# A transformer layer on one core: branch B's sums as a list of small jobs, its last additions as accumulating transfers, and another order of its products

## The chip, the cores and the metric

The kernel runs on one core of a Trainium2 chip. TensorE (PE) multiplies matrices and transposes, VectorE (DVE) and ScalarE (ACT) work element by element, GpSimd (POOL) here issues transfers, and SyncE (SP) issues most of the loads. The metric is the device time of one execution in microseconds (us).

## The reference

One layer of a streaming encoder: 512 positions, width 2048, float32. Two branches, gated DeltaNet attention (A) and a convolution module (B), are mixed by learned gates; then come an output product and a per-layer embedding. What matters here is the middle:

```python
u = jax.nn.silu(layernorm(u, ln_g[i], ln_b[i])) * jax.nn.silu(z_b)
y_b = u @ w_br_b[i]
...
gate_a, gate_b = jnp.split(jax.nn.sigmoid(gate_logits + b_gate[i]), N_BRANCHES, axis=-1)
mixed = (gate_a * y_a + gate_b * y_b) @ w_out[i]
x = x + rmsnorm(mixed, g_post[i])
```

Here `u` and `y_b` are 512 x 2048, and both weights 2048 x 2048.

## The kernel before

**Numbers.** Every float32 operand of a product is split into a high part (a rounded copy, made by ScalarE: L126 for weights, L1303 for activations, L1553 for the output's weights) and a low part (what is left, a subtraction on VectorE: L127, L1305, L1554). A product is three matmuls: low activations by high weights and high by low, beside high by high (L1415, L1417, L1419 in branch B; L1572 to L1574 in the output stage).

**Seven products for eight.** Branch B, as the gates and the output product, multiplies 2 x 2 blocks with seven products instead of eight (P1, P2, P3, Q4, Q5, P6, P7), by sums of blocks. Sums of weights (`wb_sums`, `wo_sums`) were formed earlier in the run. Sums of activations (S1 to S4, each of four tiles 128x512) are formed by VectorE from the normalised tiles `ur` at the end of `layer_norm` (L1262, into `usf`) and split by L1303 and L1305. A half of the 2048 output columns is a `jp`, 0 or 1, so there are 14 products, each of 48 matmuls of 128x512: eight weight pieces (a high and a low part of 128x512), by two blocks of 128 positions, by three matmuls.

**Order.** `b_job` queues a product, or two that take turns piece by piece. The program before runs P1 of both halves together, then P2 of both, Q4 of both, then for each half Q5, P6, P7, P3. After every matmul of a product `tick()` advances generators that are spawned beside the products: `norm` (the layer norm and the sums, resumed by it every fourth tick, and run to its end by `finish("norm")` ahead of the first Q5) and `mix`. The weights are prepared some pieces ahead. The engines run their own queues in program order.

**Results.** A product's two results lie in PSUM tiles `yp`, all from `yps`, a pool of four banks. When a product ends, its function is called at once and issues all its work in a row: `snap_b` copies a result to SBUF (L1429, ScalarE), `tt_b` adds and subtracts results (L1433, VectorE), and `fin_b` multiplies a finished result by the gate (L1291) and adds it into the mix (L1294). The mix is 16 tiles of 128x512, `gt` in the trace, and already holds branch A's part (L1158, `evac_ya`, which evicts branch A's last results). The `gate_in` function loads the gates (L1287, SP).

**Turning the mix.** `mix` transposes the finished mix for the output product: `turned` (L1318, four transposes of 128x128 on TensorE into `tp`), `combine_low` for the low half of the columns (it forms the operand `ah`, `al` and the sum `sf`, L1333 and L1334) and `combine_high` for the high half (L1303, L1305, L1349, L1353, L1357). Each waits until `added` counts four blocks for its column. Mix columns are numbered 0 to 3; `combine_low(k2)` reads column k2 // 2, `combine_high(k2)` column k2 // 2 + 2.

**Output stage.** Then the output weights come by SP (L1536), are split into `wsp`, and multiplied (L1572 to L1574). Part of their buffers (`rw`) lie in memory that branch B's results used until then. Results go to PSUM banks of three pools in turn (`bank`).

Of the kernel before, what the change touches and what calls it, by code (L numbers as in the profile page):

```python
# [15 lines left out]
P = 128  # L16
# [65 lines left out]
def _body(ctx, tc, A, out):  # L82
# [1107 lines left out]
    def layer_norm():  # L1190
# [59 lines left out]
        us1, us3 = [None] * 4, [None] * 4  # L1250
        for name in ("S1", "S2", "S3", "S4"):
            for k2 in range(4):
                if name == "S1":
                    us1[k2] = hp("usf")
                elif name == "S3":
                    us3[k2] = hp("usf")
                t = us3[k2] if name == "S3" else us1[k2]
                for kk, c in halves(k2):
# [3 lines left out]
                    nc.vector.tensor_tensor(t[:, c], a, b, op)  # L1262
                yield 4
                uS[name][k2] = sw_split(*((s2, "s2") if name == "S1" else (hpool, "h") if name == "S3" else (lop, "lop")), t)
                yield 6
# [23 lines left out]
    def fin_b(tts, j, cs):  # L1289
        for tt, c in zip(tts, cs):  # L1290
            nc.vector.tensor_tensor(c, c, gate_b[tt][j], ALU.mult)  # L1291
        for tt, c in zip(tts, cs):
            m = mixed[tt][j]
            nc.vector.tensor_tensor(m, m, c, ALU.add)  # L1294
            added[j] += 1

# [17 lines left out]
    def turned(kk):  # L1314
        ps = gps.tile([P, T], F32, tag="g", name="tp")
        for tt in range(NTT):
            c = (kk % 4) * P
            nc.tensor.transpose(ps[:, tt * P:(tt + 1) * P], mixed[tt][kk // 4][:, c:c + P], ident)  # L1318
        return ps

    def combine_low(k2):
        while added[k2 // 2] < NTT:
            yield
        ah = hpool.tile([P, T], F32R, tag="h", name="ah")
        al = hpool.tile([P, T], F32R, tag="h", name="al")
        s3_ = hpool.tile([P, T], F32, tag="h", name="sf")
        for kk, c in halves(k2):
# [5 lines left out]
            nc.vector.tensor_tensor(al[:, c], cm[kk][:, LO], ah[:, c].bitcast(F32), ALU.subtract)  # L1333
            nc.vector.tensor_tensor(s3_[:, c], cm[kk][:, LO], cm[kk][:, HI], ALU.subtract)  # L1334
# [4 lines left out]
    def combine_high(k2):  # L1339
        while added[k2 // 2 + 2] < NTT:  # L1340
            yield
# [19 lines left out]
    def split_mixed():  # L1361
        for part in (combine_low, combine_high):
            for k2 in range(4):
                yield from part(k2)

    def split_s3():
        for k2 in range(4):
            AW["S3"][k2] = sw_split(s3, "s3", Sf.pop(k2))
# [10 lines left out]
    def b_opnd(name, kk, t):  # L1379
# [12 lines left out]
    b_banks = [0]  # L1392

    def b_bank():
        b_banks[0] += 1
        return yps.tile([P, T], F32, tag="y", name="yp")
# [502 lines left out]
```

## Time and profile before

| | us |
|---|---|
| median of 3 runs | 2441.44 (2440.29 to 2443.78) |
| the profiled execution | 2441.21 |
| its span | 2439.4 |
| branch B's first matmul | 1899.59 |
| the output stage's first matmul | 2082.82 |
| the second output product's first matmul | 2100.45 |
| mean granted TensorE clock | 0.995 |

The profile counts an engine as busy while an instruction of it runs. A row of the timeline has the start, the duration, the engine, the line, the operation, the tile written and those read, and in brackets the idle time before it with the tile, engine and line that ended it. A row with x2 joins two instructions that follow each other. A few matmul records are missing from the trace, so a gap in the list with no bracket is not idle time. A matmul's duration is longer than the distance to the next start, since matmuls are pipelined; the distance is the pace.

### The profile page before, as it was taken

Reading aid. Unit: us, or ns where it says so; the run is one execution under the profiler, and the core shown is the slowest. Engines: PE = TensorE matmul, PEld = TensorE weight load, DVE = VectorE, ACT = ScalarE, POOL = GpSimd, SP = SyncE. Lnnn points to the kernel's source line nnn. Section 1 sums busy time; section 2 is a strip of 40 time slices with the busy share of each in tenths; the row PEclk is TensorE's granted clock in tenths of the full one; section 3 lists DMA queues with packets and bytes.
Section 4 is the critical chain, followed back from the end, with each engine's and each line's share of the span. In section 5 each row is a group of like instructions: output and inputs, shape, how many; then the busy total and the mean of one; then the engine's idle time right before and its main releaser. Section 6 shows DMA issues by size and latency. Waiting matters only on the chain. (4 is left out here: it accounts for less than half of the span.)

```text
span 2439.4 us, 33786 instructions
## 1 busy us (share of the span) xinstructions
PE 2399.4 (98%) x11870; PEld 1972.0 (81%) x11870; DVE 1877.9 (77%) x3500; ACT 1206.9 (49%) x2409; POOL 496.5 (20%) x513
## 2 busy tenths in 40 slices
PE   9999999999999999999999999999999899999998
PEld 7888888887788888888888887888887687787886
DVE  8878878776778677776868778999998868867644
ACT  6455545554554545445454544544325554644532
POOL 1001110011112112111212213998730000000000
PEclk9999999999999999999999999999999999999999
DMA  7576776664366565556565453533534465764652
GB/s 273 171 201 189 212 200 206 202 164 167 131 173 185 165 186 144 189 151 173 153 193 173 130 170 94 160 128 105 179 116 164 147 207 182 258 204 146 211 175 76
DMA packets 142234, 417.96 MB, mean 171 GB/s; under 512 B 16240, under 2 KB 24688, under 8 KB 141040
## 3 DMA queue, kind: packets, MB, share of 16 engines
q1 hardware_dynamic: 120304, 327.71, 39.8%
q0 software_dynamic: 19456, 83.90, 14.9%
q10 hardware_dynamic: 2304, 4.20, 0.5%
q8 instruction: 93, 1.52, 0.2%
q14 instruction: 77, 0.63, 0.1%
HBM read 384.28 MB, written 98.57 MB: 198 GB/s over the span
## 5 line engine op out<-in xcount | busy, mean ns | idle before, releaser
L126 ACT CAST w<-raw 128x512 fp32r<-128x512 f32 x628 | 385.9, 618 | 495.9 <-PE g L187 261.5
L185 PE MATMUL g<-hl,w 128*128 128x512 f32 x1536 | 610.5, 397 | 0.0
L187 PE MATMUL g<-hh,w 128*128 128x512 f32 x1536 | 608.2, 396 | 0.0
L183 PE MATMUL g<-hh,w 128*128 128x512 f32 x1536 | 608.1, 396 | 0.0
L127 DVE TENSOR_TENSOR w<-raw,w 128x512 fp32r<-128x512 f32 x514 | 355.1, 698 | 148.6 <-ACT w L126 146.3
L185 PEld LDWEIGHTS g<-hl,w 128*128 128x128 f32 x1536 | 289.0, 188 | 55.4 <-issue 1.4
L183 PEld LDWEIGHTS g<-hh,w 128*128 128x128 f32 x1536 | 289.2, 188 | 54.1
L187 PEld LDWEIGHTS g<-hh,w 128*128 128x128 f32 x1536 | 289.1, 188 | 54.0 <-POOL w L127 0.3
L1011 DVE SCALAR_TENSOR_TENSOR uc<-up,vec,uc 128x497 f32<-128x497 f32 (+29 forms) x390 | 282.3, 734 | 13.2 <-ACT uc L990 1.9
L127 POOL TENSOR_TENSOR w<-raw,w 128x512 fp32r<-128x512 f32 x114 | 146.6, 1299 | 58.0 <-ACT w L126 57.6
L710 DVE SCALAR_TENSOR_TENSOR cv<-g,vec,cv 128x511 f32<-128x511 f32 x144 | 106.6, 740 | 41.1 <-ACT cv L708 40.8
L1149 PE MATMUL yp<-w,oh 128*128 128x512 f32 x256 | 100.1, 391 | 0.0
L1151 PE MATMUL yp<-w,ol 128*128 128x512 f32 x256 | 99.5, 391 | 0.0
L1147 PE MATMUL yp<-w,oh 128*128 128x512 f32 x256 | 99.1, 389 | 0.0
L898 DVE TENSOR_TENSOR prod<-UT,VT 128x2 f32<-128x2 f32 (+30 forms) x248 | 87.2, 352 | 6.5
L1516 POOL TENSOR_TENSOR rmsm<-totm,mhalf_c 128x2 f32<-128x2 f32 x2 | 2.1, 1040 | 386.2 <-DVE totm L1514 386.2
L1033 POOL TENSOR_TENSOR uc<-uc,pr 128x511 f32<-128x511 f32 (+29 forms) x60 | 75.9, 1265 | 8.3 <-ACT pr L1032 7.7
L1748 PE MATMUL f<-w,xh 128*128 128x512 f32 x192 | 75.1, 393 | 1.0 <-DVE xl L1669 1.0
L1749 PE MATMUL f<-w,xh 128*128 128x512 f32 x192 | 75.1, 391 | 0.3 <-DVE w L127 0.3
L1573 PE MATMUL f<-wsp,opl 128*128 128x512 f32 x192 | 75.3, 392 | 0.0
L1572 PE MATMUL f<-wsp,oph 128*128 128x512 f32 x192 | 75.1, 391 | 0.0
L1750 PE MATMUL f<-w,xl 128*128 128x512 f32 x192 | 74.9, 390 | 0.0
(424 smaller groups left out, 5029.9 us busy)
## 6 DMA issues: line engine op xcount, KB each, us to landing
raw<-in_w_in SPq DMA_DIRECT2D x194, 512.0 KB, 3.4
wb_sums<-in_w_br_b POOLq DMA_DIRECT2D x48, 512.0 KB, 7.3
wo_sums<-in_w_out POOLq DMA_DIRECT2D x48, 512.0 KB, 8.0
raw<-in_w_ple_gate SPq DMA_DIRECT2D x40, 512.0 KB, 4.0
raw<-in_w_br_a SPq DMA_DIRECT2D x32, 512.0 KB, 3.4
raw<-wb_sums SPq DMA_DIRECT2D x32, 512.0 KB, 3.9
raw<-in_w_ga SPq DMA_DIRECT2D x24, 512.0 KB, 4.8
raw<-in_w_gb SPq DMA_DIRECT2D x24, 512.0 KB, 4.8
```

What stands on the lines that cost most here:

```text
L126: nc.scalar.copy(hi, rq)
L127: low_part[0].tensor_tensor(lo, rq, hi.bitcast(F32), ALU.subtract)
L183: mm(ps, wh, rh, start=(k == 0), stop=False)
L185: mm(ps, wh, rl, start=False, stop=False)
L187: mm(ps, wl, rh, start=False, stop=(k == NK - 1))
L710: nc.vector.scalar_tensor_tensor(y[:, s:], ps[:, 0:T - s], vv(w0 + 3 - s), y[:, s:], ALU.mult, ALU.add)
L898: pin(nc.vector.tensor_tensor(pv_, um, vm, ALU.mult))
L1011: pin(nc.vector.scalar_tensor_tensor(y[:, s:], u[:, 0:T - s], vv(w0 + TAPS - 1 - s), y[:, s:], ALU.mult, ALU.add))
L1033: pin(nc.gpsimd.tensor_tensor(y[:, s:], y[:, s:], pr[:, s:], ALU.add))
L1147: mm(ps[tt], lh[:, b], wh, start=k == 0, stop=False)
L1149: mm(ps[tt], lh[:, b], wl, start=False, stop=False)
L1151: mm(ps[tt], ll[:, b], wh, start=False, stop=k == NK - 1)
```

## The change

1. The sums of activations are no longer formed by `layer_norm` but by `form(name)`, which puts eight entries on a list, `chores`: for each of four tiles one that forms the sum (L1276) and issues ScalarE's copy (L1278), and one that subtracts (L1285). S1 and S2 are put there when the layer norm ends, S3 after P2, S4 after the second Q5.
2. Every operation on results on VectorE goes to that list too (`chore`, L1324, and `gated`, L1318). `do_chores`, spawned with period 6, takes one entry for every six matmuls, which is one weight piece. ScalarE's copies (`snap_b`) stay where they were.
3. The addition into the mix (L1294) goes; `gated` issues an accumulating DMA of 128x512 from GpSimd's queue in its place (L1319), 16 in all.
4. The products run in another order: P1 of both halves together, then P2(0), P2(1), Q5(0), P6(0), Q5(1), P7(0), P6(1), P3(0), Q4(0), P7(1), P3(1), Q4(1). Six of them take their banks from the pools `gps` and `ups` (`HOME`).
5. `combine_low` runs in the order k2 = 2, 3, 0, 1 once P3(0) has ended, with 30 matmuls more for the first; all four `combine_high` wait for `ending`, that is for branch B's end. The output stage's PSUM banks come in another order (`bank`).

```diff
+        form("S1")
+        form("S2")
+
+    chores = deque()
+
+    def do_chores():
+        while True:
+            if chores:
+                chores.popleft()()
+            yield
...
+        home = {"S1": (s2, "s2"), "S2": (lop, "lop"), "S3": (hpool, "h"), "S4": (s2, "s2")}[name]
+        two = {}
...
+                    pin(nc.vector.tensor_tensor(t[:, c], a, b, op))
+                two[k2] = t, home[0].tile([P, T], F32R, tag=home[1], name="oph")
+                nc.scalar.copy(two[k2][1], t)
+            return f
+
+        def rest(k2):
+            def f():
+                t, hi = two.pop(k2)
+                lo = home[0].tile([P, T], F32R, tag=home[1], name="opl")
+                pin(nc.vector.tensor_tensor(lo, t, hi.bitcast(F32), ALU.subtract))
+                uS[name][k2] = hi, lo
+            return f
+        for k2 in range(5):
+            if k2 < 4:
+                chores.append(total(k2))
+            if k2 > 0:
+                chores.append(rest(k2 - 1))
...
-    def fin_b(tts, j, cs):
-        for tt, c in zip(tts, cs):
-            nc.vector.tensor_tensor(c, c, gate_b[tt][j], ALU.mult)
-        for tt, c in zip(tts, cs):
-            m = mixed[tt][j]
-            nc.vector.tensor_tensor(m, m, c, ALU.add)
+    def gated(tt, j, c):
+        def f():
+            pin(nc.vector.tensor_tensor(c, c, gate_b[tt][j], ALU.mult))
+            nc.gpsimd.dma_start(mixed[tt][j], c, accum_op=ALU.add)
             added[j] += 1
+        chores.append(f)
+
+    def chore(dst, a, b, op):
+        chores.append(lambda: pin(nc.vector.tensor_tensor(dst, a, b, op)))
...
+        if k2 == 2:
+            yield 30
...
-        while added[k2 // 2 + 2] < NTT:
+        while not ending:
...
-        for part in (combine_low, combine_high):
-            for k2 in range(4):
-                yield from part(k2)
+        for k2 in (2, 3, 0, 1):
+            yield from combine_low(k2)
+        for k2 in range(4):
+            yield from combine_high(k2)
...
-            next(norm)
+            if chores:
+                chores.popleft()()
+            else:
+                next(norm)
...
+    HOME = {n: p for p, ns in (((gps, "g"), (("P1", 0), ("Q5", 0), ("P6", 1))), ((ups, "u"), (("P2", 1), ("P7", 0), ("P7", 1)))) for n in ns}
...
+                pool, tag = HOME.get((pr, jp), (yps, "y"))
+                of[pr, jp] = [pool.tile([P, T], F32, tag=tag, name="yp") for _ in range(2)]
...
-        b_job([(0, "P1"), (1, "P1")], p1, [(S2_, LOW, 0), (S2_, LOW, 2)])
-        b_job([(0, "P2"), (1, "P2")], p2)
-        b_job([(0, "Q4"), (1, "Q4")], q4)
-        jobs.append(lambda: finish("norm"))
-        for jp in range(2):
-            b_job([(jp, "Q5")], q5(jp))
-            b_job([(jp, "P6")], p6(jp), [(LO_, HIGH, 2 * jp + 1), (LO_, HIGH, 2 * jp)])
-            b_job([(jp, "P7")], p7(jp))
-            b_job([(jp, "P3")], p3(jp), [(LO_, LOW, 2 * jp + 1)])
...
+        def p6(jp, ps):
+            u = b_u["u2", jp] = b_u["s1", jp]
+            d = b_u["d", jp] = [unit(HP_, "bd") for _ in ps]
+            for t in range(2):
+                chore(u[t], ps[t], u[t], ALU.add)
+            for t in range(2):
+                chore(d[t], b_u["s5", jp][t], u[t], ALU.subtract)
+
+        def p7(jp, ps):
+            u, s5 = b_u["u2", jp], b_u["s5", jp]
+            for t in range(2):
+                chore(u[t], ps[t], u[t], ALU.add)
+            for t in range(2):
+                chore(s5[t], s5[t], u[t], ALU.subtract)
+            gate_all(HIGH, 2 * jp + 1, s5)
...
+        def q4(jp, ps):
+            u = b_u["u2", jp]
+            for t in range(2):
+                chore(u[t], ps[t], u[t], ALU.add)
+            gate_all(HIGH, 2 * jp, u)
+            while jp and chores:
+                chores.popleft()()
+
+        jobs.append(lambda: spawn(do_chores(), 6, "chores"))
+        b_job([(0, "P1"), (1, "P1")], keep("s1", lambda jp: HP_))
+        b_job([(0, "P2")], p2, [(S2_, LOW, 0), (S2_, LOW, 2)])
+        b_job([(1, "P2")], p2)
+        s5 = keep("s5", lambda jp: HP_ if jp else S2_)
+        b_job([(0, "Q5")], s5, [(S2_, HIGH, 1)])
+        b_job([(0, "P6")], p6)
+        b_job([(1, "Q5")], s5)
+        b_job([(0, "P7")], p7, [(S2_, LOW, 1)])
+        b_job([(1, "P6")], p6, [(HP_, HIGH, 0)])
+        b_job([(0, "P3")], p3, [(LO_, HIGH, 3)])
+        b_job([(0, "Q4")], q4)
+        b_job([(1, "P7")], p7, [(LO_, LOW, 3)])
+        b_job([(1, "P3")], p3, [(LO_, HIGH, 2)])
+        b_job([(1, "Q4")], q4)
...
-        if banks[0] % 8 < 2:
+        n = banks[0]
+        kind = "uuffffuu"[n] if n < 8 else "ffffgguu"[n % 8]
+        if kind == "u":
             return ups.tile([P, T], F32, tag="u", name="f")
-        if banks[0] % 8 < 6:
+        if kind == "f":
```

What VectorE runs when branch B begins, before, and then now (`gt` is the mix, `ur` a normalised tile, `usf` a sum, `w` a weight piece):

```order
L1262 TENSOR_TENSOR usf<-ur 128x256
L1247 TENSOR_TENSOR ul<-ur,uh 128x512
L1231 TENSOR_TENSOR ur<-ur,rstd_ps 128x512 x2
L1158 TENSOR_TENSOR gt<-yp,gt 128x512
L1236 TENSOR_TENSOR ur<-ur,zb 128x512 x2
L1158 TENSOR_TENSOR gt<-yp,gt 128x512
L1247 TENSOR_TENSOR ul<-ur,uh 128x512
L1158 TENSOR_TENSOR gt<-yp,gt 128x512
L1247 TENSOR_TENSOR ul<-ur,uh 128x512
L1231 TENSOR_TENSOR ur<-ur,rstd_ps 128x512
L127 TENSOR_TENSOR w<-raw,w 128x512 x2
L1236 TENSOR_TENSOR ur<-ur,zb 128x512
```

```order
L1158 TENSOR_TENSOR gt<-yp,gt 128x512
L1247 TENSOR_TENSOR ul<-ur,uh 128x512
L1158 TENSOR_TENSOR gt<-yp,gt 128x512
L1247 TENSOR_TENSOR ul<-ur,uh 128x512
L1231 TENSOR_TENSOR ur<-ur,rstd_ps 128x512 x2
L1158 TENSOR_TENSOR gt<-yp,gt 128x512
L1236 TENSOR_TENSOR ur<-ur,zb 128x512 x2
L127 TENSOR_TENSOR w<-raw,w 128x512
L1247 TENSOR_TENSOR ul<-ur,uh 128x512
L127 TENSOR_TENSOR w<-raw,w 128x512
L1247 TENSOR_TENSOR ul<-ur,uh 128x512
L1231 TENSOR_TENSOR ur<-ur,rstd_ps 128x512
```

The sum (L1262) is gone from ahead of the weight splits (L127), the evictions of branch A's results (L1158) stand earlier, and both splits now stand ahead of the last L1231, with one subtraction (L1247) between them.

What VectorE runs when the first half's P7 ends, before, and then now (`bsnap` and `bd` are results kept in SBUF, `gb` a gate):

```order
L1433 TENSOR_TENSOR bsnap<-yp,bsnap 128x512
L127 TENSOR_TENSOR w<-raw,w 128x512
L1433 TENSOR_TENSOR bsnap<-bsnap 128x512 x2
L1291 TENSOR_TENSOR bsnap<-bsnap,gb 128x512 x2
L1433 TENSOR_TENSOR bd<-bsnap 128x512
L1294 TENSOR_TENSOR gt<-gt,bsnap 128x512
L1433 TENSOR_TENSOR bsnap<-yp,bsnap 128x512
L1294 TENSOR_TENSOR gt<-gt,bsnap 128x512
L1433 TENSOR_TENSOR bsnap<-bsnap 128x512 x2
L1291 TENSOR_TENSOR bsnap<-bsnap,gb 128x512 x2
L1294 TENSOR_TENSOR gt<-gt,bsnap 128x512 x2
L127 TENSOR_TENSOR w<-raw,w 128x512 x5
```

```order
L127 TENSOR_TENSOR w<-raw,w 128x512 x2
L1324 TENSOR_TENSOR bsnap<-yp,bsnap 128x512 x2
L127 TENSOR_TENSOR w<-raw,w 128x512 x2
L1324 TENSOR_TENSOR bsnap<-bsnap 128x512 x2
L127 TENSOR_TENSOR w<-raw,w 128x512 x2
L1318 TENSOR_TENSOR bsnap<-bsnap,gb 128x512 x2
L127 TENSOR_TENSOR w<-raw,w 128x512 x4
L1324 TENSOR_TENSOR bsnap<-yp,bsnap 128x512 x2
L127 TENSOR_TENSOR w<-raw,w 128x512 x2
L1324 TENSOR_TENSOR bd<-bsnap 128x512 x2
L127 TENSOR_TENSOR w<-raw,w 128x512 x6
L1324 TENSOR_TENSOR bd<-yp,bd 128x512 x2
```

Fourteen operations of 128x512 stood behind one split; now at most two stand between splits, the additions into `gt` are gone, and the multiplications by the gate are now L1318.

What VectorE runs when the output stage opens, before, and then now (`wsp` is a piece of the output's weights, `rw` and `raw` its buffers, `cm` the turned low half of the mix, `sf` a sum of it):

```order
L1305 TENSOR_TENSOR opl<-sf,oph 128x512
L1291 TENSOR_TENSOR bd<-bd,gb 128x512
L1357 TENSOR_TENSOR sf<-tp,sf 128x256 x2
L1291 TENSOR_TENSOR bd<-bd,gb 128x512
L1294 TENSOR_TENSOR gt<-gt,bd 128x512
L1305 TENSOR_TENSOR opl<-sf,oph 128x512
L1305 TENSOR_TENSOR opl<-tp,oph 128x512 x2
L1349 TENSOR_TENSOR sf<-cm,tp 128x256 x2
L1294 TENSOR_TENSOR gt<-gt,bd 128x512
L1554 TENSOR_TENSOR wsp<-raw,wsp 128x1024
L1305 TENSOR_TENSOR opl<-sf,oph 128x512
L1554 TENSOR_TENSOR wsp<-raw,wsp 128x1024
```

```order
L1324 TENSOR_TENSOR bsnap<-yp,bsnap 128x512 x2
L1318 TENSOR_TENSOR bsnap<-bsnap,gb 128x512 x2
L1610 TENSOR_TENSOR wsp<-raw,wsp 128x1024 x2
L1334 TENSOR_TENSOR opl<-sf,oph 128x512 x3
L1610 TENSOR_TENSOR wsp<-rw,wsp 128x1024
L1334 TENSOR_TENSOR opl<-sf,oph 128x512
L1610 TENSOR_TENSOR wsp<-raw,wsp 128x1024
L1610 TENSOR_TENSOR wsp<-rw,wsp 128x1024
L1334 TENSOR_TENSOR opl<-tp,oph 128x512 x2
L1383 TENSOR_TENSOR sf<-cm,tp 128x256 x2
L1610 TENSOR_TENSOR wsp<-rw,wsp 128x1024
L1334 TENSOR_TENSOR opl<-sf,oph 128x512
```

Before, two additions into the mix (L1294) and the operations of a first `combine_high` (L1305, L1349) lie between the last results and the second weight piece; now two weight pieces stand right behind the four operations on the last results, and the first `combine_high` (L1334, L1383) begins behind the fifth.

More of the change, by code (lines that the diff above doesn't have):

```diff
@@ L1332, in combine_low @@
             nc.scalar.copy(ah[:, c], cm[kk][:, LO])
[L1333 to L1334 removed]
+            yield 4
+            pin(nc.vector.tensor_tensor(al[:, c], cm[kk][:, LO], ah[:, c].bitcast(F32), ALU.subtract))
+            pin(nc.vector.tensor_tensor(s3_[:, c], cm[kk][:, LO], cm[kk][:, HI], ALU.subtract))
             yield
@@ L1361, in split_mixed @@
     def split_mixed():
-        for part in (combine_low, combine_high):
-            for k2 in range(4):
-                yield from part(k2)
+        for k2 in (2, 3, 0, 1):
+            yield from combine_low(k2)
+        for k2 in range(4):
+            yield from combine_high(k2)
     def split_s3():
         for k2 in range(4):
+            while k2 not in Sf:
+                next(mix)
             AW["S3"][k2] = sw_split(s3, "s3", Sf.pop(k2))
```

100 lines of the change are left out of this document (43 added, 57 removed).

## The prediction, made before the changed kernel ran

> **What bounds the kernel now.** I read the page first, then the busy time in 10 us windows through the part that the change touches, then TensorE's own timeline there, and last what VectorE was doing at each gap.
>
> ```profile
> PE 2399.4 (98%) x11870; PEld 1972.0 (81%) x11870; DVE 1877.9 (77%) x3500; ACT 1206.9 (49%) x2409; POOL 496.5 (20%) x513
> 1910.00:1920.00 10.00, 7.70 (x31) 5.38 (x30) 10.00 (x21) 6.46 (x12) 0.00 (x0) 1.00 0.83 252
> 1930.00:1940.00 10.00, 5.95 (x20) 4.68 (x20) 8.44 (x19) 5.33 (x10) 0.00 (x0) 0.83 0.39 138
> 1940.00:1950.00 10.00, 10.00 (x46) 8.27 (x45) 5.00 (x8) 4.68 (x8) 0.00 (x0) 1.00 0.53 174
> 2070.00:2080.00 10.00, 7.12 (x25) 5.04 (x24) 10.00 (x18) 3.83 (x6) 0.00 (x0) 0.83 0.27 80
> ```
>
> The columns of a window are its length, the busy time of PE, PEld, DVE, ACT and POOL, TensorE's granted clock, the DMA share and GB/s. TensorE is the bound: 2399.4 of 2439.4 us, so 40 us are idle in the whole run. Where its windows fall below 10 (7.70, 5.95, 7.12), VectorE is at 10.00 or was until the gap; where VectorE is at 5.00, TensorE is full. So in this stage TensorE loses time to bursts on VectorE, not to a shortage of VectorE time as such: it is idle half of 1940 to 1950. TensorE's timeline (start, duration, [idle before <- what ended it]) says what each gap waits for:
>
> ```profile
> 1899.59 0.39 PE L1415 MATMUL yp<-w,uh 128*128 128x512 f32 x1
> 1903.64 0.50 PE L1415 MATMUL yp<-w,uh 128*128 128x512 f32 x1 [2.53 <-DVE gt L1158]
> 1919.72 0.74 PE L1419 MATMUL yp<-w,uh 128*128 128x512 f32 x2 [1.54 <-DVE w L127]
> 1934.11 0.50 PE L1415 MATMUL yp<-w,uh 128*128 128x512 f32 x1 [4.05 <-ACT bsnap L1429]
> 1936.49 0.63 PE L1417 MATMUL yp<-w,ul 128*128 128x512 f32 x1
> 1936.92 0.63 PE L1419 MATMUL yp<-w,uh 128*128 128x512 f32 x1
> 1944.03 0.39 PE L1415 MATMUL yp<-w,uh 128*128 128x512 f32 x1
> 1955.37 0.39 PE L1419 MATMUL yp<-w,uh 128*128 128x512 f32 x1
> 2074.24 0.44 PE L1318 MATMUL tp<-cst,gt 128*128 128x128 f32 x2 [2.70 <-DVE gt L1294]
> 2082.82 0.39 PE L1572 MATMUL f<-wsp,ah 128*128 128x512 f32 x1
> 2091.44 0.50 PE L1574 MATMUL f<-wsp,ah 128*128 128x512 f32 x1 [3.96 <-DVE wsp L1554]
> 2100.45 0.39 PE L1572 MATMUL f<-wsp,oph 128*128 128x512 f32 x1
> ```
>
> Undisturbed pace: 50 matmuls lie between the starts at 1944.03 and 1955.37, so one takes 11.34/50 = 0.2267 us. After a gap of 2.5 us and more the clock is lower for some 3 us (0.43 us from 1936.49 to 1936.92), which adds about 2 us to it; no such stretch follows the gap of 1.54.
>
> ```profile
> L1415 PE MATMUL yp<-w,oph 128*128 128x512 f32 x128 | 50.9, 397 | 0.0
> L1415 PE MATMUL yp<-w,uh 128*128 128x512 f32 x96 | 38.8, 407 | 6.6 <-ACT bsnap L1429 4.1 <-DVE gt L1158 2.5
> L1318 PE MATMUL tp<-cst,gt 128*128 128x128 f32 x64 | 10.0, 281 | 6.2 <-DVE gt L1294 6.0 <-DVE sf L1357 0.2
> 2101.03 1.07 PE L1318 MATMUL tp<-cst,gt 128*128 128x128 f32 x8 [0.19 <-DVE sf L1357]
> 2101.85 0.48 PE L1573 MATMUL f<-wsp,opl 128*128 128x512 f32 x1
> ```
>
> This gives a ledger. L1415, L1417 and L1419 have 128 + 96 = 224 matmuls each, 672 in all: 14 products of 48, 10.88 us each. Eight transposes lie between 2101.03 and 2101.85, 0.10 us each; 40 of the 64 stand in branch B. First stage (P1 of both halves): 1899.59 to 1934.11 is 34.5 us for 96 matmuls, 21.8: **12.8 lost**. The other 12 products: 1934.11 to 2082.82 is 148.7 for 130.6 + 4.1: **14.0 lost**. First output product: 2082.82 to 2100.45 is 17.6 for 10.88 + 0.8: **5.9 lost**. Together 32.7 us; later windows are full, so this is all the change can win.
>
> **The change part by part.** *First stage.* What VectorE does when the stage begins:
>
> ```profile
> 1894.36 0.42 DVE L1262 TENSOR_TENSOR usf<-ur 128x256 f32<-128x256 f32 x1
> 1898.03 0.68 DVE L1158 TENSOR_TENSOR gt<-yp,gt 128x512 f32<-128x512 f32 x1
> 1898.63 1.28 DVE L1236 TENSOR_TENSOR ur<-ur,zb 128x512 f32<-128x512 f32 x2
> 1905.91 0.68 DVE L1158 TENSOR_TENSOR gt<-yp,gt 128x512 f32<-128x512 f32 x1
> 1908.47 1.28 DVE L127 TENSOR_TENSOR w<-raw,w 128x512 fp32r<-128x512 f32 x2
> ```
>
> A full tensor_tensor holds VectorE for 0.60 us (1898.03 to 1898.63), a half one 0.34. Four small sums (L1262) leave the queue ahead of the weight splits, 1.4 us, and the last L1158 no longer stands in a cluster right before them. I walk the new order with these durations from 1894.36: the first weight's low part is done near 1905.9 and the next near 1907.1, against 1909.1 and 1909.7 before. P1(0) takes PSUM banks of another pool, so the 2.53 at 1903.64 goes, and TensorE has used up its prepared weights after some 24 matmuls, near 1905. It then waits about 1.8 for the first new pair and 1.4 for the second; from there a pair of splits comes each 2.4 us (two splits and two listed operations), and TensorE needs 2.72 for it. With half a slow stretch, 1.3, this is 4.5 lost. P2(0) takes the two of yps' four banks that P1(1) leaves, and P2(1) those of ups, so the 4.05 at 1934.11 goes. **Loss 4.5, bounds 2 and 9**: 2 is the first wait alone; 9 is both waits grown past 2.5, with two slow stretches.
>
> *The other twelve products.* The burst that is taken apart:
>
> ```profile
> 2066.29 1.28 DVE L1433 TENSOR_TENSOR bsnap<-yp,bsnap 128x512 f32<-128x512 f32 x2
> ...
> 2068.69 1.28 DVE L1291 TENSOR_TENSOR bsnap<-bsnap,gb 128x512 f32<-128x512 f32 x2
> 2069.89 1.28 DVE L1294 TENSOR_TENSOR gt<-gt,bsnap 128x512 f32<-128x512 f32 x2
> ...
> 2074.71 1.28 DVE L127 TENSOR_TENSOR w<-raw,w 128x512 fp32r<-128x512 f32 x2
> ```
>
> For 8.4 us no weight is split, and the transposes wait 2.70 for its end. Now each six matmuls (1.36 us) bring one split and at most one listed operation, 1.20 us, so VectorE keeps up. The list has 76 operations, 16 of them in P1's 16 pieces; 60 remain for the 96 pieces of twelve products. Per product VectorE then has 4.8 us of splits and 3.0 of the list in 10.88; in P7(1) and P3(1) the work behind the early transposes joins, some 9.9 of 10.88. The 16 additions into the mix (16 x 0.60 = 9.6 us) leave VectorE for GpSimd's queue, which is empty here (POOL 0.00 above). Each product's banks are read at least one product before they are taken again. The gate loads on SP wait for buffers read long before. The transposes no longer stand right behind an addition: the four groups for mix column 1 come 34 matmuls (7.7 us) after the last gate multiplication for it is queued, those for column 0 some 11.3 us. **Loss 2, bounds 0 and 6**: 6 is one more wait of 2.7 with its slow stretch at the start of P7(1), and 1.3 of small ones.
>
> *The opening of the output stage.*
>
> ```profile
> 2080.36 1.23 DVE L1554 TENSOR_TENSOR wsp<-raw,wsp 128x1024 fp32r<-128x1024 f32 x1
> 2087.70 1.29 DVE L1305 TENSOR_TENSOR opl<-tp,oph 128x512 fp32r<-128x512 f32 x2 [0.33 <-ACT oph L1303]
> 2088.91 0.74 DVE L1349 TENSOR_TENSOR sf<-cm,tp 128x256 f32<-128x256 f32 x2
> SPq L1536 <- DVE gt L1294: 8.3, 1, 8.3
> 2090.33 0.33 SPq L1536 DMA_DIRECT2D rw<-in_w_out  x1
> raw<-wb_sums SPq DMA_DIRECT2D x32, 512.0 KB, 3.9
> ```
>
> Before, SP's next weight load stood 8.3 us behind the last L1294 and went out at 2090.33, 7.5 us after the stage began; the third weight split is what TensorE waited for (3.96). Now that load waits for the last gate multiplication: with X the stage's start, VectorE empties banks and multiplies from X+0.4 to X+2.8 (four operations), the load goes out at X+2.9, lands after about 4 (3.9 is the median of the last row, a load of the same size), and the weight that uses it is split by X+9.1, needed at X+9.5. Against it: all four high parts of the mix are now split here, three before. One costs 1.2 + 0.67 + 0.6 + 0.67 + 0.6 + 0.67 + 0.6 = 5.0 us on VectorE. Over three output products TensorE takes 3 x 11.7 = 35 us, and VectorE has twelve splits of 1.14, four times 5.0 and 2.4: 36. So slack is about 1 us at each weight. **Loss 2, bounds 0.5 and 6** (as before).
>
> *Transfers that carry the additions.* The trace has 16 of the same kind and size on the same queue, earlier in the run:
>
> ```profile
> L419 POOL DMA_DIRECT2D zt<-in_w_gb x16: 862/868/1177, 413.0 to 512.7; - x16
> 413.00:513.00 100.00, 100.00 (x443) 82.77 (x443) 82.59 (x134) 49.13 (x82) 13.49 (x16) 1.00 0.72 198
> DMA to landing us min/median/max: 3.6/5.7/8.8
> ```
>
> The last row is of all accumulating transfers of that line. Issue 0.87 us, landing 5.7, at most 8.8, with DMA busier (0.72) than branch B's windows from 1930 on. Their source there is DRAM and here SBUF, which the trace does not show; I take 5.7, bounds 3.6 and 16 (one landing, and two behind each other at 8). Margins, less 0.3 for the multiplication: 7.4 us at the first transposes, 11.0 at column 0, and in the opening, whose first transposes stand 36 matmuls into the stage (X+9.0 with a wait) against gates done at X+2.8, 5.9. So 5.7 costs nothing; 8.8 costs 1.4 + 2.9 = 4.3.
>
> The Trainium skill, "SBUF — State Buffer", section "SBUF: two separate sides", speaks against this: GpSimd's descriptors are written through a port pair that some VectorE operations lock, and a transfer of 620 ns took 3100. By that figure each issue would be 2.2 us longer, an estimate from the page: landing 7.9, 0.5 + 2.0 = 2.5 lost, 2419.5 us. The issues above, with VectorE 82.59 busy, show 862 to 1177 ns, so here the trace disagrees with it and the sum stays without it.
>
> *Sum.* 4.5 + 2 + 2 = 8.5 lost of 32.7, so 24.2 saved. Of the profiled execution's 2441.2 us (span 2439.4), which stands 0.2 below the median of 2441.44: **2417.0**. All lower bounds, 2.5, give 2411; all upper ones, 21, give 2429.5.
>
> **The rivals.** *First stage unchanged.* VectorE at 10.00 from 1910 to 1930 speaks for it: if splitting and listed operations still fill it, the whole 12.8 stay, other waits taking the place of the two that go: 8.3 more than 4.5, 15.9 saved, 2425. Against it: the L1262 and L1305 work there is now rationed by TensorE's own pace. *Opening overloaded.* VectorE needs 36 of 35 us; if the fourth high part comes first and the third split behind it, 5.0 more and half a slow stretch: 6 more, 2423. *The other side: accumulating transfers land late.* Each first-reading group stands in TensorE's queue, and every matmul behind it waits. With landing L the stalls are (L - 7.4) + (L - 11.0) + (L - 5.9) and three slow stretches of 2. This eats 24.2 from L = 14.2 on; at L = 16 it is 8.6 + 5.0 + 10.1 + 6 = 29.7, hence 2447, slower. For it: an unknown source, two or four transfers queued together. Against it: no landing above 8.8 in the busier stretch. *The list does not spread.* If VectorE's listed operation waits for a product that TensorE has not ended, the splits behind it wait, and each product's end costs the 1.5 of small waits again: 12 x 1.2 = 14 in place of 2, 2429. Against it: splits run some pieces ahead of their use.
>
> **How the numbers follow.** Forecast 0.62; first stage unchanged 0.12; opening overloaded 0.11; list does not spread 0.05; late landings 0.10, of which 0.06 reach slower and the rest falls between. A measurement of this kernel tells a difference from about 0.2%, 4.9 us. Faster by more: 0.62 + 0.12 + 0.11 + 0.05 less 0.05 for mishaps that add up, 0.85; within: 0.08; slower: 0.07. The range 2410 to 2431 takes the forecast's bounds and three rivals.
>
> **What would show it.** First stage: no wait of TensorE on L1158 or on the evictions of P1, and about 26 us from its first to its last matmul. Middle: no run of more than two listed operations on VectorE without a split, 10.9 to 11.3 us a product. Opening: the weight load issued about 3 us into the stage, first output product under 14 us. Landings: the accumulating transfers near 6 us and no transposes waiting for them. I am wrong if transposes wait on these transfers, if TensorE waits on L127 in the middle products, or if the first output product still takes over 16 us.

## The result, and the profile after

The changed kernel takes 2424.45 us (median of 6 runs, 2422.44 to 2426.65), the kernel before 2441.91 in the same series. The ratio is 0.9929 with a 95% interval of 0.9916 to 0.9942: 17.5 us faster, by 0.7%. The prediction said 2417.0 and 2410 to 2431. So the direction and the range held, and 6.7 of the forecast 24.2 us did not come. The profiled execution took 2426.65 us (span 2424.8), which is the slowest of the six, 2.2 above the median. What follows is read from it: its span is 14.6 us shorter than before, not 17.5.

The page's busy line and the same four windows, of the changed kernel:

```profile
PE 2392.9 (99%) x11870; PEld 1969.7 (81%) x11870; DVE 1869.5 (77%) x3484; ACT 1204.7 (50%) x2405; POOL 511.1 (21%) x529
1910.00:1920.00 10.00, 8.66 (x31) 7.06 (x32) 10.00 (x20) 5.81 (x10) 0.00 (x0) 0.83 0.45 147
1930.00:1940.00 10.00, 10.00 (x46) 8.28 (x45) 5.99 (x10) 4.59 (x8) 0.00 (x0) 1.00 0.71 237
1940.00:1950.00 10.00, 10.00 (x45) 8.26 (x45) 7.07 (x11) 4.82 (x8) 1.85 (x2) 1.00 0.81 207
2070.00:2080.00 10.00, 5.76 (x24) 4.50 (x23) 5.96 (x9) 4.73 (x6) 0.00 (x0) 0.76 1.03 355
```

The hole at 1930 is closed. In the last window TensorE is still low, but now VectorE is low with it (5.96) and the DMA engines are full (1.03): VectorE no longer bounds this stretch. TensorE's timeline, the rows that carry the ledger and all tagged waits from branch B's start to the second output product, in order of time:

```profile
1899.69 0.39 PE L1456 MATMUL yp<-w,uh 128*128 128x512 f32 x1
...
1906.09 0.73 PE L1460 MATMUL yp<-w,uh 128*128 128x512 f32 x2 [1.70 <-DVE w L127]
...
1911.34 1.18 PE L1460 MATMUL yp<-w,uh 128*128 128x512 f32 x2 [2.22 <-DVE w L127]
...
2029.64 0.55 PE L1347 MATMUL tp<-cst,gt 128*128 128x128 f32 x3 [1.60 <-DMA gt<-bd]
...
2063.94 0.39 PE L1628 MATMUL f<-wsp,ah 128*128 128x512 f32 x1
...
2072.76 0.33 PE L1347 MATMUL tp<-cst,gt 128*128 128x128 f32 x1 [0.25 <-DMA gt<-bsnap]
2077.07 1.33 PE L1347 MATMUL tp<-cst,gt 128*128 128x128 f32 x5 [3.98 <-DMA gt<-bsnap]
...
2082.77 0.39 PE L1628 MATMUL f<-wsp,oph 128*128 128x512 f32 x1
```

No product waits for a PSUM bank any more. The ledger by the prediction's pace: branch B runs from 1899.69 to 2063.94, 164.25 us for 152.4 of matmuls and 3.2 of 32 transposes, 8.6 lost. Of these, 6.1 lie in the first stage (each start there less the one before, over 0.2267 a matmul, summed: two waits with 4.2 and a slow stretch of 1.7 behind the second) and 2.5 in the twelve products. The first output product takes 18.83 for 11.7: 7.1 lost. From its end to the span's end there are 342.0 us against 339.0; 0.8 of that is eight transposes that stood in branch B before. TensorE's tagged waits in that last part sum to 4.8 against 2.4, with this one on top, in the next stage's second matmul line:

```profile
PE f L1807 <- DVE w L127: 2.3, 1, 2.3
```

| lost, us | before | forecast | after |
|---|---|---|---|
| first stage | 12.8 | 4.5 | 6.1 |
| other twelve products | 14.0 | 2 | 2.5 |
| first output product | 5.9 | 2 | 7.1 |
| behind it (more than before) | 0 | 0 | 2.3 |

Together 18.0 us are lost where the forecast had 8.5. The opening became slower than it was before the change.

The accumulating transfers, all 16, by their line (issue in ns: shortest, median, longest; then the landing):

```profile
L1319 POOL DMA_DIRECT2D gt<-bsnap x8: 862/877/1159, 2000.8 to 2066.4; - x8
L1319 POOL DMA_DIRECT2D gt<-bc x4: 857/1070/1197, 1943.8 to 1955.2; - x4
L1319 POOL DMA_DIRECT2D gt<-bd x4: 862/1014/1165, 2020.1 to 2059.7; - x4
DMA to landing us min/median/max: 3.8/6.8/10.6
```

Their issue is as short as that of the earlier ones (857 to 1197 ns here, 862 to 1177 there). Their landing is what came out longer than the 5.7 taken: 6.8 in the middle and 10.6 at most. The Trainium skill ("SBUF — State Buffer", section "SBUF: two separate sides") has its 3100 ns for a transfer beside a VectorE `tensor_copy`, and says that `tensor_tensor` did not stall one. The trace agrees: all that VectorE runs around these issues, and in the prediction's window from 413 to 513, is TENSOR_TENSOR. So the prediction misread the Trainium skill where it made each issue 2.2 us longer by it and then found the trace in disagreement; no run here puts a copy beside an issue. What the trace shows late is the landing.

### The profile page after: what moved, and what is told of

The parts are those of the page before. It is cut to its first block, busy times and chain, and to the rows that moved or that the text cites. A ratio compares the mean times of both kernels' runs of the same rounds, so it can differ in the third digit from the quotient of the medians.

```text
span 2424.8 us, 33810 instructions
## 1 busy us (share of the span) xinstructions
PE 2392.9 (99%) x11870; PEld 1969.7 (81%) x11870; DVE 1869.5 (77%) x3484; ACT 1204.7 (50%) x2405; POOL 511.1 (21%) x529
## 4 chain that ended last, share of the span: by engine, by line
PE 88%; issue 5%; DVE 3%; DMA 2%; ACT 1%; POOL 1%; SPq 0%; POOLq 0%; DVEq 0%; ACTq 0%
PE g L185 14%; PE g L187 14%; PE g L183 14%; PE zp L473 6%; PE zp L472 6%; PE zp L471 6%; PE yp L1151 2%; PE yp L1149 2%; PE yp L1147 2%; PE f L1629 2%; PE f L1628 2%; PE f L1630 2%; PE f L1806 2%; PE f L1808 2%; PE f L1807 2%
## 5 line engine op out<-in xcount | busy, mean ns | idle before, releaser
L126 ACT CAST w<-raw 128x512 fp32r<-128x512 f32 x628 | 385.2, 618 | 490.5 <-PE g L187 261.5
L127 DVE TENSOR_TENSOR w<-raw,w 128x512 fp32r<-128x512 f32 x514 | 355.3, 699 | 142.5 <-ACT w L126 140.1
L127 POOL TENSOR_TENSOR w<-raw,w 128x512 fp32r<-128x512 f32 x114 | 146.9, 1305 | 57.9 <-ACT w L126 57.6
L721 POOL COPY kq<-kc 128x512 f32<-128x512 f32 x16 | 11.5, 721 | 310.6 <-ACT kc L719 172.7
L1628 PE MATMUL f<-wsp,oph 128*128 128x512 f32 x192 | 75.1, 391 | 0.0
L1630 PE MATMUL f<-wsp,oph 128*128 128x512 f32 x192 | 74.9, 390 | 0.0
```

The source lines that it names most:

```text
L126: nc.scalar.copy(hi, rq)
L127: low_part[0].tensor_tensor(lo, rq, hi.bitcast(F32), ALU.subtract)
```

## The experiments

Twelve kernels, each an edit of the changed kernel, in three series, each timed beside the kernel before, whose median was 2441.71, 2440.95 and 2441.62 us in them. The changed kernel itself was timed in the series of the result only (2424.45 beside 2441.91), so differences from it are good to about a microsecond.

**1. The last two additions on VectorE.** Only for the last product, Q4 of the second half:

```diff
+            if tt < 2 or j != 2:
                 nc.gpsimd.dma_start(mixed[tt][j], c, accum_op=ALU.add)
                 added[j] += 1
+        def g():
+            m = mixed[tt][j]
+            pin(nc.vector.tensor_tensor(m, m, c, ALU.add))
+            added[j] += 1
...
+        if tt >= 2 and j == 2:
+            chores.append(g)
```

> As the changed kernel, but the two additions behind the last product, Q4 of the second half, run on VectorE and not as accumulating transfers. Theory A (the opening lost some 5 us because its first transposes waited for these two transfers, which landed late among the weight loads): the transposes no longer wait, the first output product takes about 13.5 us in place of 18.8, and the time is about 2419.5 us. Rival B (the output's weights are what comes late there, and the transposes only stood in front): TensorE waits some 4 us for a weight piece instead, and the time is 2423 to 2425 us.

Measured: 2418.54 us (2418.0 to 2420.1), ratio 0.9905 (0.9892 to 0.9919). TensorE's timeline where the first transposes of the opening stand, all rows that wait:

```profile
2070.86 1.04 PE L1355 MATMUL tp<-cst,gt 128*128 128x128 f32 x8
...
2072.45 0.50 PE L1636 MATMUL f<-wsp,ah 128*128 128x512 f32 x1 [0.56 <-ACT wsp L1617]
```

The eight transposes run in one row with no wait in front; the wait for a weight piece that comes to light behind them is 0.56 us. The first output product takes 13.3 us in place of 18.8. Theory A holds: without these two transfers the median falls by 5.9 us.

**2. All 16 additions on VectorE**, each as an entry of its own on the list:

```diff
-            nc.gpsimd.dma_start(mixed[tt][j], c, accum_op=ALU.add)
-            added[j] += 1
+        def g():
+            m = mixed[tt][j]
+            pin(nc.vector.tensor_tensor(m, m, c, ALU.add))
+            added[j] += 1
         chores.append(f)
+        chores.append(g)
```

> As the changed kernel, but all 16 additions run on VectorE as list entries of their own, one per six matmuls. Theory A: the opening gains as with the last two alone, and the wait of 1.6 us at the first transposes goes too; the list has 92 entries in 112 pieces and keeps up: about 2418 us, a few us under the changed kernel. Rival C (taking 9.6 us of additions off VectorE is what the gain rests on): splits and transposes wait for VectorE again at the end of branch B, over 4 us of new waits, 2427 us or more.

Measured: 2418.74 us (2417.59 to 2419.8), ratio 0.9905 (0.9892 to 0.9919). The waits of TensorE in branch B and the first output product are the first stage's 3.9, one of 0.7 for a weight piece in the opening, and none of a transpose. Rival C falls: with all 16 additions back on VectorE the time is that of experiment 1, where 14 are transfers (2418.74 and 2418.54). Once the work is spaced, the 9.6 us that the transfers take off VectorE are worth nothing, since the list has room for them.

**3. The list without its spacing.** Every entry is taken as soon as it is there:

```diff
         while True:
-            if chores:
+            while chores:
                 chores.popleft()()
             yield
...
-        jobs.append(lambda: spawn(do_chores(), 6, "chores"))
+        jobs.append(lambda: spawn(do_chores(), 1, "chores"))
```

> As the changed kernel, but every entry of the list is taken as soon as it is there, so that the work of a product's end stands in a row on VectorE, as before the change; banks, order of products and accumulating transfers stay. Theory D (the spacing is what wins the middle products): TensorE waits for weight splits behind each burst, 1 to 2 us at most product ends, in all some 8 to 14 us, 2433 to 2438 us. Rival E (banks, order and the transfers win it, the prepared pieces cover a burst of up to four operations): under 3 us more, 2424 to 2428 us.

Measured: 2436.1 us (2433.57 to 2437.83), ratio 0.9976 (0.9967 to 0.9985): 11.7 us over the changed kernel. The size is theory D's, the way only partly. TensorE's waits in this kernel, in us, times and the longest (rows of the changed kernel's own size left out):

```profile
PE yp L1460 <- DVE w L127: 5.7, 6, 2.2
...
PE tp L1347 <- DMA gt<-bd: 3.2, 1, 3.2
...
PE yp L1456 <- ACT w L126: 1.6, 1, 1.6
```

Branch B takes 174.6 us against 164.25, 10.35 more. Splits behind bursts cost 1.8 (5.7 against 3.9); 1.0 of this is in the first stage, so theory D's 1 to 2 us at most product ends did not come. A weight that came late costs 1.6. Some 4.5 lie at the first transposes: they wait 3.2 in place of 1.6 for a transfer, and a slow stretch that costs some 3 us follows, which did not follow the 1.60. The remaining 2.4 or so are small and were not taken apart. The transposes stand nearer to their transfer here. The code queues them 30 matmuls after the last list entry of their mix column has been taken, and a burst takes the entries at once. The issue of this transfer, in the changed kernel and then in this one:

```profile
2020.08 1.77 POOL L1319 DMA_DIRECT2D gt<-bd  x2 [17.47 <-DVE bd L1318]
```

```profile
2023.26 1.77 POOL L1319 DMA_DIRECT2D gt<-bd  x2 [21.92 <-DVE bd L1318]
```

TensorE began to wait for it at 2028.0 in the changed kernel, 8.0 us after the issue, and at 2028.2 here, 5.0 after it. So the spacing wins in two ways: fewer splits and weights come late, and the transposes stand farther behind their transfers. What it would win in a kernel without the transfers, no run shows.

**4. Two entries for every six matmuls:**

```diff
-        jobs.append(lambda: spawn(do_chores(), 6, "chores"))
+        jobs.append(lambda: spawn(do_chores(), 3, "chores"))
```

> The changed kernel with one list entry for every three matmuls in place of six: a split of 0.60 and two entries of 0.60 for 1.36 us of TensorE's, 1.80, so VectorE falls behind by 0.44 a piece while the list lasts, at most 6 entries or three pieces at a product's end. Theory N (the prepared pieces cover a lag of 1 to 2 us): within 2 us of the changed kernel, 2423 to 2427 us. Rival O (the spacing must keep VectorE under TensorE's pace at each piece): some of the 12 us that the undivided bursts cost comes back, 2428 to 2432 us.

Measured: 2430.1 us (2429.36 to 2431.62), ratio 0.9955 (0.9939 to 0.9972). Rival O holds: half of what the undivided bursts cost comes back at a pace of two, though the list is the same. TensorE waits five times for a split, 5.7 in all (3.9 in the changed kernel), and 2.5 for the transfer of P3 (1.6 there).

**5. All products in the one pool of four banks:**

```diff
-    HOME = {n: p for p, ns in (((gps, "g"), (("P1", 0), ("Q5", 0), ("P6", 1))), ((ups, "u"), (("P2", 1), ("P7", 0), ("P7", 1)))) for n in ns}
+    HOME = {}
```

> As the changed kernel, but all products take their banks from the one pool of four, as before. Theory F (banks of other pools removed the two bank waits of the first stage): the wait of 2.5 us at the second P1 and one of some 4 us at the first P2 come back with their slow stretches, and list entries that read a bank late hold up further products: 8 us or more, 2432 us and up. Rival G (the spread only matters at the first P2): 4 to 6 us, 2428 to 2431 us.

Measured: 2423.7 us (2422.91 to 2424.59), ratio 0.9926 (0.9913 to 0.9938). Both theories fall: the spread of the banks is worth nothing. No wait for a bank comes back. The rows of ScalarE say why, first of the kernel before, then of this one, around the end of P1:

```profile
1932.95 0.62 ACT L1303 CAST oph<-usf 128x512 fp32r<-128x512 f32 x1 [1.43 <-DVE usf L1262]
1933.48 2.04 ACT L1429 COPY bsnap<-yp 128x512 f32<-128x512 f32 x4
```

```profile
1924.94 0.59 ACT L1471 COPY bsnap<-yp 128x512 f32<-128x512 f32 x1 [0.78 <-PE yp L1460]
...
1926.99 1.26 ACT L1471 COPY bsnap<-yp 128x512 f32<-128x512 f32 x2
```

Before, the four copies that empty the banks stood on ScalarE behind a copy of a sum, and that waited for VectorE's sum (L1262); P2 waited for all of it. Now TensorE itself is what the first copy waits for. The bank wait at P2 was VectorE's queue seen through ScalarE's, and with the sums rationed it goes without another bank.

**6. Q4 ahead of P3 in the second half**, all transfers kept:

```diff
-        b_job([(1, "P7")], p7, [(LO_, LOW, 3)])
-        b_job([(1, "P3")], p3, [(LO_, HIGH, 2)])
-        b_job([(1, "Q4")], q4)
+        b_job([(1, "P7")], p7, [(LO_, HIGH, 2)])
+        b_job([(1, "Q4")], q4, [(LO_, LOW, 3)])
+        b_job([(1, "P3")], p3)
```

(The loop that empties the list at branch B's end moves from `q4` to `p3`.)

> The changed kernel with all 16 accumulating transfers, but Q4 of the second half runs ahead of P3 of it. The two transfers that the output stage's first transposes read then go out a product, 10.9 us, earlier; the ones behind P3 are read by the third pair of transposes only. Theory A (what costs in the opening is the distance between a transfer's issue and its first reader, not the transfer): the wait of 4.2 us goes with its slow stretch, the first output product takes about 13.3 us, and the time is 2418 to 2419 us, as with the two additions on VectorE. Rival (the transfers themselves slow the weight loads there): a weight piece is waited for instead, 2422 us or more.

Measured: 2418.81 us (2416.74 to 2419.06), ratio 0.9905 (0.9889 to 0.9922). The landings are as long as ever, and TensorE waits for none of them, as this answer on the transfers and TensorE's row in the opening show:

```profile
DMA to landing us min/median/max: 3.3/6.6/10.4
```

```profile
2069.98 1.04 PE L1347 MATMUL tp<-cst,gt 128*128 128x128 f32 x8
```

The first output product takes 11.8 us, which is its pace with no loss. So the opening's loss was the distance from a transfer's issue to its first reader. One product in between covers a landing of 10.4.

**7. Fewer weight loads at once in the opening:**

```diff
-        if n < 3 or n % 8 in (1, 4, 7):
+        if n < 7 or n % 8 in (1, 4, 7):
             raw = rawp.tile([P, 1024], F32, tag="raw", name="raw", bufs=3)
```

> The changed kernel with all its accumulating transfers, but the first seven loads of the output's weights go through the three raw buffers, so that fewer of them are under way when the last two transfers are issued. Theory L (a transfer lands late when it shares the DMA engines with a row of weight loads): the last two land within 7 us in place of about 10, and the transposes wait under 1.5 us for them; the weights may come later themselves, so the time says little, 2419 to 2426 us. Rival M (their source in SBUF, or two behind each other on one queue, makes them slow): landing near 10 us and a wait of 4 us as in the changed kernel.

Measured: 2423.66 us (2421.53 to 2425.15), ratio 0.9928 (0.9913 to 0.9943). Inconclusive: the last two transfers land at a median of 8.5 us, as they did (8.7), and the transposes wait 3.1 for them (4.2 in the changed kernel), but the DMA engines are as full as before (1.02 in the window around them), so the edit did not take away what it was to take away. What the changed kernel shows by itself is two pairs of transfers, the windows around them (the last column but one is the DMA share), and then their landing in the same windows:

```profile
2048.00:2059.00 11.00, 11.00 (x54) 9.04 (x53) 9.01 (x18) 6.57 (x14) 1.74 (x2) 1.00 0.72 192
2064.00:2077.00 13.00, 8.84 (x40) 6.86 (x38) 9.50 (x13) 6.17 (x8) 1.76 (x2) 0.93 1.01 298
```

```profile
gt<-bsnap POOLq DMA_DIRECT2D x2, 256.0 KB, 4.8
...
gt<-bsnap POOLq DMA_DIRECT2D x2, 256.0 KB, 8.7
```

The source in SBUF is the same and so is the size; the pair in the quieter window (0.72) landed after 4.8, the one in the full window (1.01) after 8.7. A source in SBUF by itself is therefore not slow. Nor is a second transfer right behind the first: two issued in a row at 2033.93 landed after 5.1. All eight pairs of this trace fit: in the order of the DMA share in windows of 9 to 13 us around them (0.72, 0.85, 0.90, 0.90, 0.92, 0.94, 0.99, 1.01) they landed after 4.8, 5.1, 5.9, 6.1, 5.9, 7.9, 9.7 and 8.7 us. No run took the load away, so that the full engines make the landing long is argued and not shown.

**8. The list opened after P1**, on top of experiment 1:

```diff
-        jobs.append(lambda: spawn(do_chores(), 6, "chores"))
         b_job([(0, "P1"), (1, "P1")], keep("s1", lambda jp: HP_))
+        jobs.append(lambda: spawn(do_chores(), 6, "chores"))
```

> As the kernel with the last two additions on VectorE, and the list is opened only after P1, so that the sums S1 and S2 leave the first stage. Theory H (what is left of the first stage's loss, about 6 us, comes half from the layer norm's own work and half from the four small sums that stand ahead of the second pair of splits): the wait of 1.7 us stays, the one of 2.2 shrinks to about 1 and its slow stretch goes, 3 us less than with the last additions alone: 2415 to 2416 us. Rival I (the sums only move: the list is now fuller by 16 entries when Q5 needs S1, and entries are forced out in a row there): new waits in the middle products take it back, 2418 us or more.

Measured: 2416.11 us (2415.43 to 2417.07), ratio 0.9898 (0.9883 to 0.9912). One row is left of the waits on splits in branch B:

```profile
PE yp L1468 <- DVE w L127: 1.7, 1, 1.7
```

The second wait of 2.2 is gone altogether and branch B takes 159.15 us in place of 162.63, 3.5 less: theory H. Of the 3.5, 1.6 is a slow stretch behind that wait, which other kernels with the same wait do not have (last section). The median moved by 2.4, and the intervals of the two ratios overlap.

**9. The old rotation of the output's banks** from the ninth bank on, on top of experiment 1:

```diff
-        kind = "uuffffuu"[n] if n < 8 else "ffffgguu"[n % 8]
+        kind = "uuffffuu"[n] if n < 8 else "uuffffgg"[n % 8]
```

> As the kernel with the last two additions on VectorE, and after the first eight the output's banks rotate as before the change (two of ups, four of fps, two of gps). Theory J (the other rotation costs some 2 us at the start of the next stage, where TensorE waits 2.3 us for a weight split that it did not wait for before): that wait shrinks below 1 and the time is 2416 to 2417 us. Rival K (that wait is due to the loads there): 2418 to 2419 us, the wait of 2.3 stays.

Measured: 2416.15 us (2415.42 to 2418.53), ratio 0.9899 (0.9885 to 0.9914). The waits at the next stage's start:

```profile
PE f L1814 <- DVE xl L1735: 1.0, 1, 1.0
...
PE f L1815 <- DVE w L127: 0.3, 1, 0.3
```

The 2.3 is 0.3 again, and a wait of 1.0 stands beside it, as in the kernel before (1.0 and 0.3). Theory J holds in all 14 traces: the nine kernels with the new rotation have the 2.3, the five with the old one 1.0 and 0.3. In experiment 1's trace the next stage's first matmuls stand among the last transposes before it, here behind them all; by which bank this comes about was not followed up. The median fell by 2.4; here too the ratios' intervals overlap.

**10 to 12. What the parts make together.** Kernel 10 joins the edits of 1, 8 and 9, kernel 11 those of 6, 8 and 9, kernel 12 those of 2, 8 and 9.

> The last two additions on VectorE, the list opened after P1, and the output's banks in the old rotation from the ninth on: the three gains measured one by one are 5.9 (last), 2.4 (list) and 2.4 us (banks). If they add up: 2413.5 to 2414 us. If two of them meet in one wait: 2416 us.

> As the kernel that joins the three gains, but all 16 additions are transfers and the swapped order of the last two products takes the place of the additions on VectorE: 2413 to 2414.5 us if distance is all that the transfers need; over 2416 if they cost something besides.

> As the kernel that joins the three gains, but all 16 additions run on VectorE, 92 entries in the 96 pieces of the twelve products. If the transfers are worth nothing once the work is spaced: 2413.5 to 2415 us. If taking 9.6 us off VectorE matters when the list is this full: new waits of TensorE for splits, 2417 us or more.

Measured, in one series with the kernel before at 2441.62:

| | median, us | range | ratio (95%) |
|---|---|---|---|
| 10: last two additions on VectorE | 2416.17 | 2415.13 to 2419.45 | 0.9899 (0.9884 to 0.9914) |
| 11: swap, all transfers | 2415.82 | 2414.34 to 2416.21 | 0.9894 (0.9879 to 0.9909) |
| 12: no transfers at all | 2414.34 | 2412.68 to 2414.82 | 0.9888 (0.9873 to 0.9903) |

The gains of 8 and 9 do not add up in kernel 10: a wait of 1.0 for a weight of branch B (on L126) and one of 0.8 in the opening have come up, and why is open. Its time is the 2416 of the second expectation, but no one wait shared by two gains was found. Kernel 11 came out between its two expectations (to 2414.5, and over 2416), so whether the transfers cost anything besides distance stays open. Kernel 12 has the lowest median, as its first expectation had it, 27.3 us under the kernel before and 10.1 under the changed one, without one accumulating transfer; the ratios' intervals of the three overlap. A fuller list (92 entries in 96 pieces) did not cost anything.

## Why the prediction was right, and where it was off

**What bounds it.** Right in the main: TensorE lost its time to rows of VectorE's work, and spreading them out wins most of it back. Undoing the spacing alone gives back 11.7 of the 17.5 us (experiment 3), and twice the pace 5.6 (experiment 4). A part of this runs over the transposes and their transfers and not over late splits, and the prediction did not have that; the other 5.8 us were not assigned to a part of the change.

**The number.** The total stayed inside the range, which allowed up to 21 us lost; the trace has 18.0. No error made up for another: all four terms came out larger than forecast. Two of the prediction's three signs of being wrong came, transposes that wait on the transfers and a first output product over 16 us (18.83); the third, a wait on L127 in the middle products, did not.

**First stage: right in size, wrong in one cause.** The walk gave waits of 1.8 and 1.4; the trace has 1.70 and 2.22, and with a slow stretch 6.1 lost in place of 4.5, inside the bounds of 2 and 9. The step "P1(0) takes PSUM banks of another pool, so the 2.53 goes" and its twin at P2 named the wrong part of the change: experiment 5 gives the banks back and both waits stay away. They had been VectorE's lateness: at P1 in evictions (L1158) that now stand earlier, at P2 by way of ScalarE's queue. The rival that this stage stays as it was does not hold: of 12.8, 6.7 went.

**The twelve products: right.** 2.5 lost for 2. The order on VectorE is the one forecast. In this stretch of its timeline, at the end of P7 of the first half, where 14 operations stood behind one split before:

```profile
1994.55 1.28 DVE L1324 TENSOR_TENSOR bsnap<-yp,bsnap 128x512 f32<-128x512 f32 x2
1995.75 1.37 DVE L127 TENSOR_TENSOR w<-raw,w 128x512 fp32r<-128x512 f32 x2
1997.04 1.29 DVE L1324 TENSOR_TENSOR bsnap<-bsnap 128x512 f32<-128x512 f32 x2
1998.24 0.68 DVE L127 TENSOR_TENSOR w<-raw,w 128x512 fp32r<-128x512 f32 x1
1999.14 0.69 DVE L127 TENSOR_TENSOR w<-raw,w 128x512 fp32r<-128x512 f32 x1 [0.22 <-ACT w L126]
1999.76 1.28 DVE L1318 TENSOR_TENSOR bsnap<-bsnap,gb 128x512 f32<-128x512 f32 x2
```

Two listed operations follow two splits, and VectorE itself waits now and then, so it keeps up. The one wait that is left, 1.60, is for a transfer, not for VectorE. It does not always come: in the traces of experiments 1, 5, 6, 7 and 8, which leave these two transfers and their readers as they are, TensorE does not wait there.

**The opening: the step that failed.** The term was 2 with bounds of 0.5 and 6, and it measured 7.1. What failed is "I take 5.7" for the landing at that place. The prediction held a DMA share of 0.72, where transfers of the 5.7 had run, against that of the kernel before: 0.39, 0.53 and 0.27 in the last three windows shown. In the changed kernel the same windows have 0.71, 0.81 and 1.03. The weight load went out even earlier than forecast, 2.2 us into the stage and not 2.9, and it and those behind it were under way together with the last two transfers: the prediction worked out the earlier loads as a gain and did not set them beside the transfers. The loads' own landing, taken as 4, was 8.3 to 9.1 for those into `rw`, at the median. The two transfers were issued 1.9 and 2.5 us into the stage and the transposes stood ready at 8.2, so a landing of 10.6 made a wait of 4.2 in all, and a slow stretch behind it. This is the rival of late landings at the one place with the least margin (5.9 against 7.4 and 11.0), and in some executions, more weakly, at a second; the forecast had priced a landing of 8.8 at 4.3 us for the whole kernel. Experiments 1 and 6 show it from two sides: without those two transfers, or with a product between them and their readers, 5.6 to 5.9 us come back. The rival of an overloaded VectorE in the opening does not hold: it idles there (5.96 of 10), and in experiment 1, without the two transfers, TensorE waits for no split of VectorE's in the first output product.

**A term that was missing: 2.3 behind the first output product.** The new rotation of the banks was listed as a change and costed at nothing; experiment 9 brings back the smaller waits of before (1.0 and 0.3 for 2.3), and the median falls by 2.4 us with them, though the intervals overlap.

**The rival on the other side** would have needed landings of 14.2 at three places; the longest was 10.6. **The list that does not spread** is what experiments 3 and 4 built: 2436.1 and 2430.1 against its 2429. Its price was a slip: it names 1.5 an end and multiplies 1.2, and 12 times 1.5 would have given 2433. Its way is not what the bursts showed: waits for splits in the twelve products were 0.8 in all.

## What to carry to other kernels

Work that follows each product is better spread at the pace at which the bound engine uses up its inputs than issued in a row: here one operation of 0.60 us per 1.36 us of TensorE was worth 11.7 us, and a pace of two lost half of it. Part of that was distance between transfers and their readers, so a kernel without such transfers may win less. A transfer that replaces an operation on a busy engine takes a short time of that engine and a long way to its reader; count the distance to the first reader against the landing under the load that stands there, not against the median elsewhere, or put another piece of work in between. And where one engine waits for a buffer, look at what stands ahead of the releasing instruction in its queue before giving it more buffers.

## What the runs showed of the hardware

Landings of the same transfer, 256 KB from SBUF to SBUF with an addition, ran from 3.3 to 10.4 us within one kernel (experiment 6), and issuing one took 0.86 to 1.2 us in the changed kernel. The pairs that landed late lay in windows with the fuller DMA engines (4.8 us at 0.72, 8.7 at 1.01). The slow clock behind a wait is not fixed by the wait's length near 2 us: behind 2.22 us in the first stage some eight matmuls ran at 0.43 us each in the changed kernel (granted clock 0.57 from 1911 to 1915), and behind 2.23 at the same place in experiment 5 none did (1.00 from 1912 to 1916). That alone is 1.7 us, where the six runs of the changed kernel lie within 4.2 us.
